# Reordering the down products of a two-layer MLA/GLA trunk's MLPs: the fifth sum second, the fourth sum fifth, one addition at high priority

## The chip, the core and the metric

The kernel runs on one core of a Trainium2 chip. The metric is the device time of one execution in microseconds (us). Three runs of the kernel before gave 1045.85 us as their median (1045.75 to 1047.25). The profile shows one further execution with its engines: PE is TensorE (matmul), PEld its weight loads, DVE is VectorE, ACT is ScalarE, POOL is GpSimd, SP is SyncE, which here issues DMAs only. Each engine works through its own instructions in a fixed order and waits on semaphores for the others.

## The reference

The reference is a decoder trunk of two layers on 512 tokens of width 1024, all in float32: layer 0 mixes with multi-head latent attention (MLA), layer 1 with gated linear attention (GLA), and each is followed by an MLP with a squared ReLU.

```
for i in range(DEPTH):                                  # DEPTH = 2
    x = x + mixer_i(rms_norm(x, norm_mix[i]))
    x = x + sq_relu_mlp(rms_norm(x, norm_mlp[i]), mlp_w_up[i], mlp_w_down[i])
return rms_norm(x, final_norm)

def sq_relu_mlp(xn, w_up, w_down):                      # 1024 -> 4096 -> 1024
    return jnp.square(jax.nn.relu(xn @ w_up)) @ w_down
```

The change lies in the two MLPs alone.

## The kernel before, in words

**Products.** Every float32 product is made of three fast matmuls: each operand is split into a rounded high part (ACT, line 110, or 844 with a sign) and a low part, the rest (DVE, line 113, or 845 with a sign), and high*high, high*low and low*high are added in PSUM. A weight block (`piece`, tiles `wh` and `wl`, four buffers each) costs ACT and DVE one instruction of 1024 columns each; a block of hidden values (`parts_of_quad`) one of 512 columns each. The hidden parts live in four rooms that are used in turn: the parts split as number n overwrite those split as number n-4, so that split waits until the product that read them is through.

**Seven products for eight.** The function `mlp` cuts the 4096 hidden columns into eight blocks (NB) of 512. The up and the down product of a block are 2 by 2 block products (halves of the width and of the tokens), done with seven block products each, from sums and differences of the quadrants, in place of eight. An up product is 24 matmuls of 256 columns (line 962), a down product 12 matmuls of 512 columns (line 971). The first block's up product is plain; then come seven steps, each doing the seven down products of block b and the seven up products of block b+1: one `step` (b = 0), in which ups and downs alternate, and six `step_in_halves` (b = 1 to 6, the middle steps), with seven ups and then seven downs. With two MLPs this makes two first steps and twelve middle steps.

**The down products.** With hidden quadrants q11, q12, q21, q22, DVE first makes q12 = q22 - q12 and q11 = q11 + q12. The results go to five sums in SBUF (`S11, S12, SU, S21, S5`). In a middle step of the kernel before the downs stand in this order: (1) q11 with d11; (2) the fourth sum: S21 += (q11 - q21) with d22; (3) q21 with d12, then S11 += e; (4) -q11 with d11 + ds1; (5) the fifth sum: S5 += (q11 - q22) with ds1; (6) q22 with d12, then S12 += e (line 1153); (7) q12 with ds3, then SU += d (line 1156). Products 2 and 5 (`onto`) copy their sum into two PSUM banks and back on ACT (line 1094). In `step` the later downs stand in a list at line 1084: -q11, q22, q12 (`down_12`), the fifth sum (`down_5`), the fourth (`down_21`).

**Loads.** When a product has read its weights for the last time, the step calls `after(name)`, and that issues the next block's DMA into the same tile: SP loads it, and for A2, S1, dS1 and dS3 POOL then adds a second block into it with an accumulating DMA (lines 940 and 951). In the last step of the second MLP `after` is `at_the_end`: it loads the last block's down weights and the final gain's row, rounds two of those weight tiles (`rounded(0)`), and adds S5 onto S12 (line 1199).

**What sets the order.** The order on the engines is not the order of the source. A planner walks the program with its own durations; whenever an engine is free it takes the ready instruction that stands first in the source (one under `tc.high_priority()` goes ahead of all others). Tiles of one tag are given out in the order of the source: a `tmp` (six buffers) or a `set` that is written later in the source is not given out before those ahead of it.

**The end.** After the last step of the second MLP, S12 is copied to PSUM (line 1248), the last hidden block is split (line 1250), the other two weight tiles are rounded (line 1253), the final gain is scaled by -0.5 (line 1255, DVE, 1024 columns), and `row` (line 1279) makes 96 matmuls in eight rows, the first of which accumulate onto the copy of S12. Only then do the final norm and the stores follow.

```
down_product(e, d12, p22, False)                    # sixth down of a middle step
DVE.tensor_tensor(S12, e, S12, ALU.add)             # line 1153
after("d12")
down_product(d, ds3, parts_of_quad(q12), False)     # seventh
...
loaded = {1: two_banks("e")}
ACT.activation(loaded[1], S12, AF.Copy)             # line 1248
```

Of the kernel before, what the change touches and what calls it, by code (L numbers as in the profile page):

```python
# [50 lines left out]
def trunk_kernel(ctx: ExitStack, tc: tile.TileContext, t_in: dict, out: bass.AP):  # L51
# [763 lines left out]
    def mlp(layer, nrm, nxt=None):  # L815
# [148 lines left out]
        def down_product(t, a, parts, start):  # L964
            wh, wl = piece(a, 2, 512)
            for tt in range(2):
                o = t[tt] if isinstance(t, list) else t[:, tt * 512 : (tt + 1) * 512]
                for k in range(2):
                    xh, xl = cut(parts, slice(None), slice(k * TH + tt * P, k * TH + (tt + 1) * P))
                    for n, (x_, w_) in enumerate(((xh, wh[:, k]), (xh, wl[:, k]), (xl, wh[:, k]))):  # L970
                        PE.matmul(o, x_, w_, start=start and k == 0 and n == 0, stop=k == 1 and n == 2, skip_group_check=True)  # L971


        def step(b, q, r, after):
            opening = nxt is not None
            (q11, q12), (q21, q22) = q

            def begun(src):
                t = two_banks("e")
                ACT.activation(t, src, AF.Copy)  # L980
                return t

            def add(total, t):
                if opening:
                    ACT.activation(total, t, AF.Copy)
                else:
                    DVE.tensor_tensor(total, t, total, ALU.add)

            def onto(tag, total, a, parts, fresh=False):
                t = two_banks(tag)  # L990
                if not fresh:
                    ACT.activation(t, total, AF.Copy)
                down_product(t, a, parts, fresh)
                ACT.activation(total, t, AF.Copy)

            A1, A2, s1 = W["A1"], W["A2"], W["S1"]
            a11, a12, s3, a22 = A1[:, :KH], A1[:, KH:], A2[:, :KH], A2[:, KH:]
            d11, d12, ds1, ds3, d22 = (W[n] for n in ("d11", "d12", "dS1", "dS3", "d22"))

            z = bank("u")  # L1000
            up_product(z, a11, "11", True)
            y = bank("u")
            ACT.activation(y, z, AF.Copy)

            d = two_banks("d")
            down_product(d, d11, parts_of_quad(q11), True)
            if opening:
                ACT.activation(S11, d, AF.Copy)
            e = two_banks("e") if opening else begun(d)

            up_product(y, a12, "21", False)
            finish(y, 0, 0, r)
            DVE.tensor_tensor(a11, s1, a11, ALU.add)

            down_product(e, d12, parts_of_quad(q21), opening)
            DVE.tensor_tensor(S11, e, S11, ALU.add)
            DVE.tensor_tensor(d11, ds1, d11, ALU.add)
            DVE.tensor_tensor(q12, q22, q12, ALU.subtract)
            DVE.tensor_tensor(q11, q11, q12, ALU.add)

            part = {"e": e}

            def down_11():
                down_product(d, d11, parts_of_quad(q11, -1.0), False)
                part["e"] = begun(d)
                DVE.tensor_tensor(d12, d11, d12, ALU.add)
                after("d11")

            def up_t2():
                up_product(z, a11, "T2", False)  # L1030
                u = part["u"] = tmp()
                ACT.activation(u, z, AF.Copy)
                DVE.tensor_tensor(a12, a11, a12, ALU.add)

            def up_t1():
                w = part["w"] = bank("u")
                up_product(w, s1, "T1", True)
                w2 = part["w2"] = bank("u")
                ACT.activation(w2, w, AF.Copy)
                after("S1")  # L1040

            def down_22():
                e = part["e"]
                down_product(e, d12, parts_of_quad(q22), False)
                add(S12, e)
                after("d12")

            def down_12():
                down_product(d, ds3, parts_of_quad(q12), False)
                add(SU, d)  # L1050
                after("dS3")
                DVE.tensor_tensor(q22, q22, q11, ALU.subtract)

            def up_22():
                w = part["w"]
                up_product(w, a12, "22", False)
                c = tmp()
                DVE.tensor_tensor(c, w, part["u"], ALU.add)
                finish(c, 0, 1, r)
                after("A1")  # L1060

            def up_t3():
                up_product(z, s3, "T3", False)
                v = tmp()
                ACT.activation(v, z, AF.Copy)
                c = tmp()
                DVE.tensor_tensor(c, part["w2"], v, ALU.add)
                finish(c, 1, 1, r)

            def down_5():  # L1070
                onto("e", S5, ds1, parts_of_quad(q22, -1.0), True)
                after("dS1")
                DVE.tensor_tensor(q21, q21, q11, ALU.subtract)

            def down_21():
                onto("d", S21, d22, parts_of_quad(q21, -1.0), opening)
                after("d22")

            def up_t4():
                up_product(z, a22, "T4", False)  # L1080
                finish(z, 1, 0, r)
                after("A2")

            for product in (up_t2, down_11, up_t1, down_22, up_22, up_t3, down_12, up_t4, down_5, down_21):
                product()

        def step_in_halves(b, q, r, after):
# [32 lines left out]
            c = tmp()  # L1120
            DVE.tensor_tensor(c, w2, v, ALU.add)
            finish(c, 1, 1, r)
            up_product(w, a12, "22", False)
            c = tmp()
            DVE.tensor_tensor(c, w, u, ALU.add)
# [4 lines left out]
            after("A2")  # L1130

            d = two_banks("d")
            down_product(d, d11, parts_of_quad(q11), True)
            e = copied(two_banks("e"), d)
            DVE.tensor_tensor(d11, ds1, d11, ALU.add)
            DVE.tensor_tensor(q12, q22, q12, ALU.subtract)
            DVE.tensor_tensor(q11, q11, q12, ALU.add)
            p21 = parts_of_quad(q21)
            DVE.tensor_tensor(q21, q21, q11, ALU.subtract)
            onto(S21, d22, parts_of_quad(q21, -1.0))  # L1140
            after("d22")
            down_product(e, d12, p21, False)
            DVE.tensor_tensor(S11, e, S11, ALU.add)
            down_product(d, d11, parts_of_quad(q11, -1.0), False)
            e = copied(two_banks("e"), d)
            DVE.tensor_tensor(d12, d11, d12, ALU.add)
            after("d11")
            p22 = parts_of_quad(q22)
            DVE.tensor_tensor(q22, q22, q11, ALU.subtract)
            onto(S5, ds1, parts_of_quad(q22, -1.0))  # L1150
            after("dS1")
            down_product(e, d12, p22, False)
            DVE.tensor_tensor(S12, e, S12, ALU.add)
            after("d12")
            down_product(d, ds3, parts_of_quad(q12), False)
            DVE.tensor_tensor(SU, d, SU, ALU.add)
# [34 lines left out]
        def at_the_end(name):  # L1191
            if name in ("d11", "S1", "d12", "dS3"):
                i = len(last_raw)
                t = by_k(comb(home[name]), 2)
                k0 = (NB - 1) * FB + i % 2 * 256
                SP.dma_start(t, w_dn[k0 : k0 + 256, i // 2 * 512 : (i // 2 + 1) * 512].rearrange("(k p) n -> p k n", p=P))
                last_raw.append(t)
            if name == "dS1":
                DVE.tensor_tensor(S12, S12, S5, ALU.add)
                t = comb(home[name])  # L1200
                SP.dma_start(t, t_in["fin_row"].to_broadcast([P, D]))
                gain.append(t)
                rounded(0)

        for b in range(NB - 1):
# [46 lines left out]
        DVE.tensor_tensor(SU, SU, S5, ALU.add)  # L1252
        rounded(1)
        gain = gain[0]
        DVE.tensor_scalar(gain, gain, -0.5, None, ALU.mult)
        stats = [sm(3) for _ in range(NT)]
        rows = {}
        for c in range(2):
            for th in (1, 0):
                total = (S11, S12, S21, SU)[2 * c + th]  # L1260
                if c == 0:
                    if th not in loaded:
                        loaded[th] = two_banks("d")
                        ACT.activation(loaded[th], total, AF.Copy)
                    o = loaded[th]
                for i in range(2):
                    cs = slice(i * 512, (i + 1) * 512)
                    if c:
                        o = bank("u")
                        ACT.activation(o, total[:, cs], AF.Copy, scale=-1.0)  # L1270
                    rows[2 * th + i, c] = total[:, cs], o if c else o[:, cs]

        def row(t, c):
            y, o = rows[t, c]
# [583 lines left out]
```

## Time and profile before

| | us |
|---|---|
| median of three runs | 1045.85 (1045.75 to 1047.25) |
| the profiled execution: its time | 1046.67 |
| the profiled execution: its span | 1044.9 |
| PE busy | 1035.0 (99%) |
| DVE busy | 876.9 (84%) |
| ACT busy | 696.8 (67%) |
| granted TensorE clock | 0.998 |

The span is the stretch from the first to the last instruction; 1.8 us of the execution's time lie around it. Times of instructions are counted from the span's start. The first MLP's first step begins at 206.79 and its middle steps run from 245.70 to 474.8; in the second MLP they begin at 745 and 785.91, and the last middle step ends at 1014.9. A line number names the place in the source; that of a helper (110, 113, 844, 845, 962, 971, 1094) stands for every caller.

### The profile page before, as it was taken

How to read it: one execution, taken by the hardware profiler on the slowest of the kernel's cores; microseconds unless marked ns; L12 is line 12 of the kernel's file. 1: busy time of each engine (PE TensorE's matmuls, PEld its weight loads, DVE VectorE, ACT ScalarE, POOL GpSimd, SP SyncE). 2: the span in 40 equal slices, each digit the busy share in tenths (PEclk: the TensorE clock that was granted, in tenths of full speed). 3: DMA queues.
4: the chain of work that ended last, by engine and by line, in shares of the span. 5: the costliest groups of instructions: out<-in, count | busy, mean ns of one | idle time of the engine just before them, and what ended most of it. 6: DMA issues, size and time to landing. Idle time of an engine off the chain costs nothing.

```text
span 1044.9 us, 15747 instructions
## 1 busy us (share of the span) xinstructions
PE 1035.0 (99%) x5966; PEld 903.9 (87%) x5966; DVE 876.9 (84%) x1340; ACT 696.8 (67%) x1122; POOL 114.3 (11%) x128
## 2 busy tenths in 40 slices
PE   9999999999999999999999999999999999999997
PEld 8788888899899899898888888888889989989986
DVE  7889977988989989989687399469798999898993
ACT  8667754577776776785445566555677677677784
POOL 8400010301101101000000000000011111110000
PEclk9999999999999999999999999999999999999999
DMA  7401235769878778644212222165488778778422
GB/s 232 122 21 41 81 95 147 224 166 215 216 191 202 178 203 202 161 136 126 77 55 82 87 74 75 48 162 147 95 241 201 185 202 198 194 191 191 111 81 81
DMA packets 120717, 149.98 MB, mean 144 GB/s; under 512 B 9568, under 2 KB 86368, under 8 KB 120512
## 3 DMA queue, kind: packets, MB, share of 16 engines
q1 hardware_dynamic: 96144, 117.76, 35.4%
q0 software_dynamic: 22400, 29.36, 18.0%
q10 hardware_dynamic: 2096, 1.84, 0.6%
q8 instruction: 47, 0.77, 0.3%
q14 instruction: 30, 0.25, 0.1%
HBM read 144.49 MB, written 4.19 MB: 142 GB/s over the span
## 4 chain that ended last, share of the span: by engine, by line
PE 94%; DVE 3%; ACT 2%; issue 0%; DMA 0%; ACTq 0%; SPq 0%; DVEq 0%
PE ps L971 25%; PE ps L962 25%; PE ps L118 10%; PE ps L120 10%; PE ps L119 10%; PE ps L1279 2%; PE ps L1240 2%; PE ps L1499 1%; PE ps L135 1%; PE ps L421 1%; PE ps L1626 1%; DVE wl L113 1%; PE ps L1766 0%; PE ps L1549 0%; PE ps L684 0%
## 5 line engine op out<-in xcount | busy, mean ns | idle before, releaser
L971 PE MATMUL ps<-wh,set 128*128 128x512 f32 x784 | 245.7, 390 | 0.3 <-ACT set L110 0.3
L110 ACT ACTIVATE wh<-wraw 128x1024 fp32r<-128x1024 f32 x139 | 146.4, 1056 | 110.2 <-PE ps L119 42.6
L113 DVE TENSOR_TENSOR wl<-wraw,wh 128x1024 fp32r<-128x1024 f32 x139 | 169.7, 1222 | 39.0 <-ACT wh L110 38.7
L971 PEld LDWEIGHTS ps<-wh,set 128*128 128x128 f32 x784 | 147.0, 188 | 30.7 <-ACT set L110 0.7
L962 PE MATMUL ps<-T,wh 128*128 128x256 f32 x896 | 154.9, 275 | 0.0
L971 PE MATMUL ps<-wl,set 128*128 128x512 f32 x392 | 152.6, 389 | 0.0
L113 DVE TENSOR_TENSOR wl<-comb,wh 128x1024 fp32r<-128x1024 f32 x112 | 136.8, 1221 | 18.5 <-ACT wh L110 18.3
L110 ACT ACTIVATE wh<-comb 128x1024 fp32r<-128x1024 f32 x112 | 118.3, 1057 | 47.6 <-issue 28.7
L962 PEld LDWEIGHTS ps<-T,wh 128*128 128x128 f32 x896 | 135.4, 188 | 0.4
L962 PE MATMUL ps<-T,wl 128*128 128x256 f32 x448 | 123.4, 275 | 0.0
L962 PE MATMUL ps<-set,wh 128*128 128x256 f32 x672 | 117.1, 276 | 0.0
L118 PE MATMUL ps<-set,wh 128*128 128x512 f32 x280 | 109.7, 392 | 0.0
L119 PE MATMUL ps<-set,wh 128*128 128x512 f32 x280 | 109.6, 392 | 0.0
L120 PE MATMUL ps<-set,wl 128*128 128x512 f32 x280 | 109.3, 391 | 0.0
L962 PEld LDWEIGHTS ps<-set,wh 128*128 128x128 f32 x672 | 102.6, 188 | 1.3
L962 PE MATMUL ps<-set,wl 128*128 128x256 f32 x336 | 92.7, 276 | 0.0
L971 PEld LDWEIGHTS ps<-wl,set 128*128 128x128 f32 x392 | 73.6, 188 | 14.7
L962 PEld LDWEIGHTS ps<-T,wl 128*128 128x128 f32 x448 | 84.1, 188 | 0.1
L962 PEld LDWEIGHTS ps<-set,wl 128*128 128x128 f32 x336 | 63.1, 188 | 0.0
L120 PEld LDWEIGHTS ps<-set,wl 128*128 128x128 f32 x280 | 52.6, 188 | 11.1
L119 PEld LDWEIGHTS ps<-set,wh 128*128 128x128 f32 x280 | 52.6, 188 | 11.1 <-DVE set L750 0.2
L118 PEld LDWEIGHTS ps<-set,wh 128*128 128x128 f32 x280 | 52.6, 188 | 10.7
(415 smaller groups left out, 2015.4 us busy)
## 6 DMA issues: line engine op xcount, KB each, us to landing
comb<-in_mlp_w_down_dram SPq DMA_DIRECT2D x74, 512.0 KB, 4.1
wraw<-in_mlp_w_up_dram SPq DMA_DIRECT2D x18, 1024.0 KB, 5.6
comb<-in_mlp_w_down_dram POOLq DMA_DIRECT2D x28, 512.0 KB, 6.5
wraw<-in_mlp_w_up_dram SPq DMA_DIRECT2D x28, 512.0 KB, 5.6
wraw<-in_gla_w_in_dram SPq DMA_DIRECT2D x12, 1024.0 KB, 5.2
comb<-in_mlp_w_up_dram SPq DMA_DIRECT2D x14, 512.0 KB, 4.4
comb<-in_mlp_w_up_dram POOLq DMA_DIRECT2D x14, 512.0 KB, 6.4
wraw<-in_mlp_w_up_dram POOLq DMA_DIRECT2D x14, 512.0 KB, 7.6
```

What stands on the lines that cost most here:

```text
L110: order(ACT.activation(hi, src, AF.Copy))
L113: lo_eng.tensor_tensor(lo, src, f(hi), ALU.subtract)
L118: PE.matmul(psum, wh, xh, start=start, stop=False)
L119: PE.matmul(psum, wh, xl, start=False, stop=False)
L120: PE.matmul(psum, wl, xh, start=False, stop=stop)
L135: PE.transpose(psum, src, ident[: src.shape[0], : src.shape[0]])
L421: PE.matmul(p, w[:, i, j * P : (j + 1) * P], x, start=start, stop=stop)
L962: PE.matmul(o, a_, x_, start=start and j == 0 and k == 0 and n == 0, stop=k == KH - 1 and n == 2, skip_group_check=True)
L971: PE.matmul(o, x_, w_, start=start and k == 0 and n == 0, stop=k == 1 and n == 2, skip_group_check=True)
L1240: PE.matmul(p, a, x, start=False, stop=k == 3 and n == 2, skip_group_check=True)
L1279: PE.matmul(o, a, b_, start=False, stop=k == 3 and n == 2, skip_group_check=True)
L1499: PE.matmul(p[:, t - t0], k[:, t * P : (t + 1) * P], moving[:, t], start=True, stop=True)
```

## The change

It has five parts, in the two MLPs:

1. In `step_in_halves` the fifth sum's product becomes the second down and the fourth sum's the fifth, with their `after("dS1")` and `after("d22")`. The fifth sum's factor is no longer made in place (q22 -= q11, then split with the sign -1): q11 - q22 is written to a new `tmp` tile `less` and split plainly. The splits for the first three downs and the three DVE instructions that they need (q12, q11, `less`) move up in the source, ahead of the sixth up product. The turns of the rooms change with the order: p1, p5, p2, -q11, q11 - q21, q22, q12.
2. The addition S12 += e after the sixth down stands under `tc.high_priority()`.
3. In `step` the list at the end of the function is reordered: `down_5` stands where `down_12` stood and the reverse; the split of -q11 is called ahead of `up_t2`; q22 -= q11 moves into `down_22`; the fourth sum uses the PSUM tile `e`.
4. In `at_the_end`, `rounded(0)` moves from the name dS1 to the name d22, so it stays behind the fifth down.
5. The scaling of the final gain moves behind the copies of the sums to PSUM.

```
@@ step
-            part = {"e": e}
+            part = {"e": e, "p11": parts_of_quad(q11, -1.0)}
             def down_11():
-                down_product(d, d11, parts_of_quad(q11, -1.0), False)
+                down_product(d, d11, part["p11"], False)
...
                 down_product(e, d12, parts_of_quad(q22), False)
+                DVE.tensor_tensor(q22, q22, q11, ALU.subtract)
                 add(S12, e)
...
-                onto("d", S21, d22, parts_of_quad(q21, -1.0), opening)
+                onto("e", S21, d22, parts_of_quad(q21, -1.0), opening)
...
-            for product in (up_t2, down_11, up_t1, down_22, up_22, up_t3, down_12, up_t4, down_5, down_21):
+            for product in (up_t2, down_11, up_t1, down_22, up_22, up_t3, down_5, up_t4, down_12, down_21):
@@ step_in_halves
             finish(c, 1, 1, r)
+            p1 = parts_of_quad(q11)
+            DVE.tensor_tensor(q12, q22, q12, ALU.subtract)
+            DVE.tensor_tensor(q11, q11, q12, ALU.add)
+            less = tmp()
+            DVE.tensor_tensor(less, q11, q22, ALU.subtract)
+            p5 = parts_of_quad(less)
+            p2 = parts_of_quad(q21)
             up_product(w, a12, "22", False)
...
-            down_product(d, d11, parts_of_quad(q11), True)
+            down_product(d, d11, p1, True)
             e = copied(two_banks("e"), d)
             DVE.tensor_tensor(d11, ds1, d11, ALU.add)
-            DVE.tensor_tensor(q12, q22, q12, ALU.subtract)
-            DVE.tensor_tensor(q11, q11, q12, ALU.add)
-            p21 = parts_of_quad(q21)
+            onto(S5, ds1, p5)
+            after("dS1")
+            down_product(e, d12, p2, False)
+            DVE.tensor_tensor(S11, e, S11, ALU.add)
             DVE.tensor_tensor(q21, q21, q11, ALU.subtract)
-            onto(S21, d22, parts_of_quad(q21, -1.0))
-            after("d22")
-            down_product(e, d12, p21, False)
-            DVE.tensor_tensor(S11, e, S11, ALU.add)
             down_product(d, d11, parts_of_quad(q11, -1.0), False)
             e = copied(two_banks("e"), d)
             DVE.tensor_tensor(d12, d11, d12, ALU.add)
             after("d11")
-            p22 = parts_of_quad(q22)
-            DVE.tensor_tensor(q22, q22, q11, ALU.subtract)
-            onto(S5, ds1, parts_of_quad(q22, -1.0))
-            after("dS1")
-            down_product(e, d12, p22, False)
-            DVE.tensor_tensor(S12, e, S12, ALU.add)
+            onto(S21, d22, parts_of_quad(q21, -1.0))
+            after("d22")
+            down_product(e, d12, parts_of_quad(q22), False)
+            with tc.high_priority():
+                DVE.tensor_tensor(S12, e, S12, ALU.add)
@@ at_the_end
                 gain.append(t)
+            if name == "d22":
                 rounded(0)
@@ the end of mlp
-        DVE.tensor_scalar(gain, gain, -0.5, None, ALU.mult)
         stats = [sm(3) for _ in range(NT)]
...
                     rows[2 * th + i, c] = total[:, cs], o if c else o[:, cs]
+
+        DVE.tensor_scalar(gain, gain, -0.5, None, ALU.mult)
```

More of the change, by code (lines that the diff above doesn't have):

```diff
@@ L1147, in step_in_halves @@
             after("d11")
-            p22 = parts_of_quad(q22)
-            DVE.tensor_tensor(q22, q22, q11, ALU.subtract)
-            onto(S5, ds1, parts_of_quad(q22, -1.0))
-            after("dS1")
-            down_product(e, d12, p22, False)
-            DVE.tensor_tensor(S12, e, S12, ALU.add)
+            onto(S21, d22, parts_of_quad(q21, -1.0))
[3 more added lines that the diff above has]
+                DVE.tensor_tensor(S12, e, S12, ALU.add)
             after("d12")
```

## The prediction

> **What bounds the kernel now.** I read the page first (busy shares and the chain that ended last), then the chain in order of time, to see where it leaves PE.
>
> ```profile
> span 1044.9 us, 15747 instructions
> PE 1035.0 (99%) x5966; PEld 903.9 (87%) x5966; DVE 876.9 (84%) x1340; ACT 696.8 (67%) x1122; POOL 114.3 (11%) x128
> PE 94%; DVE 3%; ACT 2%; issue 0%; DMA 0%; ACTq 0%; SPq 0%; DVEq 0%
> ```
>
> ```profile
> 209.68 2.54 PE ps L971 x11
> ...
> 212.79 1.01 ACT xT L1008
> ...
> 214.78 1.23 DVE wl L113
> 216.00 0.61 DVE tmp L859
> 216.64 0.64 ACT set L860
> 217.27 0.53 ACT set L110
> 217.84 0.72 PE ps L971 x2
> ...
> 322.18 19.09 PE ps L962 x168
> 341.27 19.07 PE ps L971 x84
> ...
> 1011.47 1.22 DVE xT L1199
> ...
> 1013.20 0.69 DVE comb L1255
> 1013.89 1.14 DVE xT L1153
> 1015.06 1.04 ACT ps L1248
> 1016.14 22.34 PE ps L1279 x96
> ```
>
> PE is 99% busy and 94% of the chain. In a middle step the chain never leaves PE: 168 up matmuls in 19.09 us (0.114 each, 2.73 a product), 84 down matmuls in 19.07 (0.227 each, 2.72 a product). In the two MLPs it leaves PE in the first step and at the end. The stretches of one step each say the same; columns are length, then busy us of PE, PEld, DVE, ACT, POOL.
>
> ```profile
> 206.79:245.70 38.91, 38.76 (x253) 35.11 (x252) 32.46 (x38) 28.50 (x38) 5.99 (x5) 1.00 0.75 185
> 322.02:360.18 38.16, 38.16 (x253) 34.85 (x252) 35.04 (x39) 28.25 (x40) 4.98 (x4) 1.00 0.76 196
> ```
>
> A middle step is 38.16 us with PE busy for all of it. So the change can win nothing in the twelve middle steps; it can only lose there. DVE has 38.16 - 35.04 = 3.1 us to spare in each. The first step takes 38.91, 0.75 more. What can be won is there and at the end.
>
> **Part 1 of the change, middle steps: forecast 0.** No matmul is added or removed. On DVE `less` takes the place of the subtraction q22 -= q11 (one of 512 columns for another), and a plain split that of a signed one. So DVE's 35.04 us stay. What moves is the time at which the parts can be made.
>
> ```profile
> 338.71 0.69 DVE L859 SCALAR_TENSOR_TENSOR tmp<-tmp,rstd 128x512 f32<-128x512 f32 x1
> ...
> 343.38 1.22 DVE L113 TENSOR_TENSOR wl<-comb,wh 128x1024 fp32r<-128x1024 f32 x1
> ...
> 351.10 0.68 DVE L845 SCALAR_TENSOR_TENSOR set<-set,set 128x512 fp32r<-128x512 f32 x1
> ```
>
> ```profile
> 343.63 0.61 PE L971 MATMUL ps<-wh,set 128*128 128x512 f32 x2
> ...
> 351.80 0.61 PE L971 MATMUL ps<-wh,set 128*128 128x512 f32 x2
> ```
>
> Each row of PE holds the last matmul of a down and the first of the next, so the second down begins at 343.86 and the fifth at 352.02. Before, the fifth's low part (line 845, 351.10 to 351.78) ends 0.7 us before its first use, the third matmul at 352.02 + 2 x 0.227 = 352.48: its room was held until the third product was through. After, the turns of the rooms follow the order of the products, so every split finds its room free at least three products (8 us) ahead. That takes a tight place away, at no gain, since PE never waited there. The new tight place is `less`: it is a `tmp`, so it comes behind the `tmp` of the fifth up's finish (338.71). At the earliest it starts at 339.32; with 0.69 for it, some 0.63 for the high part on ACT and 0.69 for the low part it is done at 341.4, and PE wants the low part at 344.31. I take 0; the other bound is the third rival below.
>
> The moved loads:
>
> ```profile
> comb<-in_mlp_w_down_dram SPq DMA_DIRECT2D x74, 512.0 KB, 4.1
> ```
>
> ```profile
> 351.78 1.19 POOL L951 DMA_DIRECT2D comb<-in_mlp_w_down_dram  x1 [11.15 <-DVE set L845]
> ```
>
> dS1's load goes up three places on SP, past d22's and d11's, and its adding DMA on POOL from 351.78 to some 342, past nothing (A2's stays ahead of it, dS3's behind). d22's load goes back three places and is wanted three products later. Each is wanted a whole step, 38 us, after its issue against 4.1 us to landing (some 10 with POOL's). Cost 0; without that cover each late us would be a us per step.
>
> **Part 3, the first steps: forecast -0.8.**
>
> ```profile
> 212.25 0.63 ACT L110 ACTIVATE set<-set 128x512 fp32r<-128x512 f32 x1 [1.10 <-PE ps L971]
> ...
> 214.78 1.23 DVE L113 TENSOR_TENSOR wl<-comb,wh 128x1024 fp32r<-128x1024 f32 x1 [1.17 <-ACT wh L110]
> ...
> 214.92 0.28 PE L962 MATMUL ps<-set,wl 128*128 128x256 f32 x1
> ...
> 217.41 0.28 PE L962 MATMUL ps<-T,wh 128*128 128x256 f32 x1
> 217.84 0.50 PE L971 MATMUL ps<-wh,set 128*128 128x512 f32 x1 [0.15 <-ACT set L110]
> ...
> 218.64 0.66 PE L971 MATMUL ps<-wh,set 128*128 128x512 f32 x2
> 758.06 0.50 PE L971 MATMUL ps<-wh,set 128*128 128x512 f32 x1 [0.18 <-ACT set L110]
> ```
>
> The split at 212.25 is that of q12, far ahead of its use: it took the room of the first down at the moment that product ended, and pushed back the copy at 212.79, the weight split behind it, the `wl` at 214.78 for which DVE sat idle 1.17, the finish (216.00), and by that q21's high part (217.27), for which PE waits at 217.84. In the new order that room goes to the split of q22 - q11, which cannot be ready so early (it needs q22's own split). The copy then starts at 212.25, 0.54 earlier, and the chain behind it by as much, until PE's own pace binds: 24 matmuls would have ended 2 x 0.114 after 217.55, and the third down matmul, at 218.64 now, could start at 217.55 + 0.23 + 2 x 0.227 = 218.23. That is 0.41, in each MLP (758.06 shows the same wait, 0.18 beside 0.15): 0.8. Bounds: 0 if another instruction fills the slot, below nothing by 0.4 in each if it is a longer one (a weight split, 1.0 for 0.6); 1.5 at most, the 0.75 over a middle step, twice. I take 0.8, the nearest to its row. The other swaps in the list cost 0: when down_5 runs, its parts, its `ds1` and the PSUM tile `e` have been ready for several products, as those of down_12 were.
>
> **Parts 2, 4 and 5, the end: forecast -1.3.**
>
> ```profile
> 1010.86 0.69 DVE L113 TENSOR_TENSOR set<-comb,set 128x512 fp32r<-128x512 f32 x1 [0.31 <-ACT set L110]
> ...
> 1012.60 0.69 DVE L113 TENSOR_TENSOR set<-set,set 128x512 fp32r<-128x512 f32 x1
> ...
> 1013.80 1.22 DVE L1153 TENSOR_TENSOR xT<-ps,xT 128x1024 f32<-128x1024 f32 x1
> ```
>
> ```profile
> 1011.20 0.63 ACT L110 ACTIVATE set<-set 128x512 fp32r<-128x512 f32 x1
> ...
> 1012.72 1.16 ACT L110 ACTIVATE set<-comb 128x512 fp32r<-128x512 f32 x2
> ```
>
> ```profile
> 1014.64 0.39 PE L971 MATMUL ps<-wh,set 128*128 128x512 f32 x1
> 1016.14 0.73 PE L1279 MATMUL ps<-set,set 128*128 128x512 f32 x2 [1.11 <-ACT ps L1248]
> ```
>
> The seventh down ends at 1014.64 + 0.23 = 1014.87; the rows of line 1279 start at 1016.14, 1.27 late, and their first two matmuls take 0.73 where two take 0.61 in the flow: 1.4 in all. They wait for the copy of S12 (1248), that for S12 += e (1153, at 1013.80), though the sixth down ended at about 1012.2 (1014.87 less 2.72). DVE had no arrears at 1010.86 (idle 0.31 before it). Ahead of 1153 stood S12 += S5 (1.13 from start to start), a hidden split (0.60) and the gain (0.61). After the change S12 += S5 follows the second down, 8 us earlier, and the gain's row, loaded at dS1, lands as much earlier, so that the planner can put the scaling into any idle slot of DVE. The hidden split then waits for its high part (1011.83) and ends its turn at 1012.47; S12 += e runs from there to about 1013.65, ACT is through with its two roundings at 1013.88, the copy ends at 1014.9, and PE goes on at 1014.95: 1.2 won, and the slow first pair with it, 1.3. If the gain still stands in front, 1013.08 and 1015.40: 0.75. Below nothing: `less` and its split bring 1.3 us more DVE work into the down phase, which has idle slots of as much; a cost of 0.5 is the bound. The high priority by itself is worth nothing that I can see: 1153 already stood first in the source among what was left, and was late only because the planner took other work until it held the sixth down to be through.
>
> **Sum.** 0 - 0.8 - 1.3 = -2.1. Against the profiled execution: 1046.67 becomes 1044.6, span 1044.9 becomes 1042.8. The median of the three runs lies 0.8 below the profiled execution; from 1045.85 I forecast 1043.7.
>
> **Rivals.** (1) Only one of the two stalls goes, because the planner fills the freed place with other work: 1045.85 - 0.8 to 1.3, so 1044.5 to 1045.1. For it: the planner is greedy and has its own durations; against: the freed places are narrow, 0.5 and 1.1 us. (2) Nothing shows: the same instructions stand before S12 += e, or new small waits eat the gain: 1045.4 to 1046.3. For it: the high priority changes no rank; against: the two instructions that stood in the way do move. (3) The other side: `less` is late in the middle steps. Line 1125, a weight split, both finishes and line 1146 stand on DVE from 339.32 to 343.38; if `less` comes behind them, its low part is done at 345.4, 1.1 after PE wants it, twelve times: +13, 1059; half the delay beyond the turning point gives 1052. It decides once `less` starts after 342.3 (344.31 less 2.0). Against it: in the source `less` stands ahead of line 1125. (4) S12 += e, drawn ahead, stands at the head of DVE before the sixth down is through, and what is queued behind it (weight splits) waits too. The row at 214.78 shows such a wait: 1.17 idle. DVE can lose 3.1 us in a step before PE starves, and a down is 2.72, so it decides only if the addition is placed more than a product too early; at 4.1 us early, 1.0 in each of twelve steps, 1058.
>
> On (4) the Trainium skill, "TensorE: Matmul & The Clock Gate", section "Architectural detail", says that the queues of ACT and DVE are strictly first in, first out. This trace agrees as far as it shows (1.17 idle with a finish behind whose product's last matmul began at 214.92). By that rule alone an early addition would block DVE, the 1058 above; by the row's 3.1 us to spare it costs nothing.
>
> **Chances.** Both stalls go (the forecast) 0.52, its own range 1043.0 to 1044.4; rival 1 0.17; rival 2 0.09; rival 3 0.18; rival 4 0.04. 0.2% is 2.1 us, about what a measurement of this kernel can tell from no change: below 1043.76 or above 1047.94. Of the forecast's 0.52 I put 0.38 below 1043.76 (little is left over if both go whole), so faster 0.38; within 0.14 + 0.17 + 0.09 = 0.40; slower 0.22. The range leaves out rivals 3 and 4 and little else: 1042.9 to 1047.0.
>
> **What would show it.** Right: no wait of line 1279 on line 1248 over 0.2 us, line 1153 starting by 1012.7 less what was won before; no wait of line 971 on line 110 in the first steps; middle steps of 38.16. Wrong: middle steps longer than 38.3 with PE waiting for a `set` at the second down (rival 3), or for `wl` (rival 4).

## The result and the profile after

The changed kernel takes 1047.64 us (median of 12 runs, 1046.1 to 1052.11); the kernel before took 1046.1 in the same session (12 runs, 1045.6 to 1047.34). The ratio is 1.0023 with a 95% interval of 1.0015 to 1.0032: slower by some 0.23%, where 0.2% faster was forecast. Beside the median the spread has changed: four of the changed kernel's runs lie at 1049 to 1052, and no run of before lies above 1047.4, here or beside a later experiment, except one slow one of 1287.51 at a granted clock of 0.752, which no comparison uses.

Three lines of the page of the changed kernel (span, busy times, shares of the chain that ended last), then the end of that chain; the profiled execution took 1047.52 us. Columns of the chain: start, length, what.

```profile
span 1045.8 us, 15773 instructions
PE 1034.9 (99%) x5966; PEld 903.4 (86%) x5966; DVE 876.6 (84%) x1340; ACT 696.5 (67%) x1122; POOL 112.9 (11%) x128
PE 93%; DVE 2%; ACT 2%; DMA 1%; issue 0%; SPq 0%; DVEq 0%; ACTq 0%
```

```profile
1009.99 1.15 DVE wl L113
...
1011.15 4.35 DMA comb<-in_mlp_w_down_dram
...
1016.06 1.02 ACT ps L1252
...
1017.12 22.27 PE ps L1284 x96
```

The work is the same (PE 1034.9 busy, 1035.0 before). What is new is a DMA in the chain that ends last: a weight split on DVE, then the load of the last weight tile, then the copy of S12 (line 1252, 1248 before), then the last product.

The stretches of the two first steps and of one middle step (length, busy us of PE, PEld, DVE, ACT, POOL; granted clock, DMA share, GB/s), first the changed kernel:

```profile
207.14:246.14 39.00, 38.80 (x254) 35.13 (x253) 32.43 (x38) 28.31 (x38) 5.97 (x5) 1.00 0.73 184
322.46:360.62 38.16, 38.16 (x254) 34.85 (x253) 34.97 (x39) 28.24 (x39) 5.11 (x5) 1.00 0.78 193
745.41:786.51 41.10, 40.90 (x272) 36.96 (x270) 33.56 (x38) 27.70 (x36) 4.99 (x4) 1.00 0.65 168
```

and the second MLP's first step in the kernel before:

```profile
744.89:785.91 41.02, 40.84 (x272) 36.97 (x270) 34.48 (x40) 29.08 (x37) 4.99 (x4) 1.00 0.64 167
```

Middle steps: 38.16 as before. First steps: 39.00 for 38.91 and 41.10 for 41.02, so 0.09 worse each in place of 0.41 better.

The end, on ACT, PE, DVE and SP's queue (in this order; the number in brackets is idle time and what ended it):

```profile
1012.90 0.63 ACT L110 ACTIVATE set<-comb 128x512 fp32r<-128x512 f32 x1 [1.71 <-DMA comb<-in_mlp_w_down_dram]
...
1015.52 0.63 ACT L110 ACTIVATE set<-comb 128x512 fp32r<-128x512 f32 x1 [0.95 <-DMA comb<-in_mlp_w_down_dram]
1016.06 1.01 ACT L1252 ACTIVATE ps<-xT 128x1024 f32<-128x1024 f32 x1
```

```profile
1015.24 0.39 PE L971 MATMUL ps<-wh,set 128*128 128x512 f32 x1
1017.12 1.20 PE L1284 MATMUL ps<-set,set 128*128 128x512 f32 x4 [1.49 <-ACT ps L1252]
```

```profile
1001.61 0.69 DVE L1276 TENSOR_SCALAR comb<-comb 128x1024 f32<-128x1024 f32 x1
...
1004.09 1.22 DVE L1202 TENSOR_TENSOR xT<-xT,sum 128x1024 f32<-128x1024 f32 x1
...
1009.90 1.22 DVE L113 TENSOR_TENSOR wl<-comb,wh 128x1024 fp32r<-128x1024 f32 x1
...
1012.95 1.23 DVE L1156 TENSOR_TENSOR xT<-ps,xT 128x1024 f32<-128x1024 f32 x1 [0.62 <-PE ps L971]
```

```profile
1011.15 0.37 SPq L1199 DMA_DIRECT2D comb<-in_mlp_w_down_dram  x1
```

S12 += e (line 1156) does start as soon as the sixth down ends, at 1012.95; it is through by 1014.18. But the copy of S12 stands on ACT behind the rounding of the last block's last weight tile, and that waits for its DMA until 1015.52. The seventh down ends at 1015.24 + 0.23 = 1015.47, PE goes on at 1017.12: 1.65 late, 1.27 before. In the kernel before that load went out at 1008.84, 5.8 us ahead of the seventh down's last matmul (1014.64):

```profile
1008.84 0.37 SPq L1196 DMA_DIRECT2D comb<-in_mlp_w_down_dram  x1
```

In the changed kernel it goes out 4.1 ahead, when the seventh down's weight split (the `wl` at 1009.90) has released the tile.

That makes 0.4 at the end and 0.2 in the first steps, against medians 1.5 apart. The experiments look for the rest.

### The profile page after: what moved, and what is told of

The parts are those of the page before. It is cut to its first block, busy times and chain, and to the rows that moved or that the text cites. A ratio compares the mean times of both kernels' runs of the same rounds, so it can differ in the third digit from the quotient of the medians.

```text
span 1045.8 us, 15773 instructions
## 1 busy us (share of the span) xinstructions
PE 1034.9 (99%) x5966; PEld 903.4 (86%) x5966; DVE 876.6 (84%) x1340; ACT 696.5 (67%) x1122; POOL 112.9 (11%) x128
## 4 chain that ended last, share of the span: by engine, by line
PE 93%; DVE 2%; ACT 2%; DMA 1%; issue 0%; SPq 0%; DVEq 0%; ACTq 0%
PE ps L971 25%; PE ps L962 25%; PE ps L118 10%; PE ps L120 10%; PE ps L119 10%; PE ps L1284 2%; PE ps L1244 2%; PE ps L1504 1%; PE ps L135 1%; PE ps L421 1%; DVE wl L113 1%; PE ps L1631 1%; DMA xT<-in_x_dram 1%; DMA comb<-in_mlp_w_down_dram 0%; PE ps L1554 0%
```

## The experiments

The kernel before was run beside each; times of different sessions differ by some tenths, so each is compared by its ratio to before in its own session. Two variants are no experiments, since the planner builds the very same program from them: the changed kernel without `tc.high_priority()`, and the changed kernel with the gain's scaling at its old place in the source. Parts 2 and 5 of the change are thus without effect; what happens at the end comes from the new order of the downs (part 1) and the hooks that move with it (part 4).

**The copy ahead of the last rounding (e1).**

```
-        ACT.activation(loaded[1], S12, AF.Copy)
+        moved = ACT.activation(loaded[1], S12, AF.Copy)
...
-        rounded(1)
+        rounded(1, (0,))                   # third tile
+        with tc.issue_after(moved.ins):    # on ACT behind the copy
+            rounded(1, (1,))               # fourth tile
```

> The changed kernel with one instruction moved: the copy of S12 to PSUM goes ahead of the rounding of the last weight tile on ACT, nothing else. Theory A (the loss sits at the end: that rounding waits for its DMA, and the copy and PE behind it): the copy starts at about 1014.2 and PE's first row of the last product within 0.3 us of the seventh down's end, where it was 1.65 late; the median falls by 1.4 to 1.8 from 1047.64, to 1045.8 to 1046.2, level with the kernel before, and the single runs of 1049 to 1052 go. Theory B (the loss sits elsewhere, in the first steps or in loads of the middle steps): the wait at the end goes as well, but the median stays at 1046.8 or more and runs above 1049 stay.

1046.32 us (11 runs, 1045.29 to 1047.55), before 1045.89; ratio 1.0004 (0.9996 to 1.0013). Its ACT rows:

```profile
1013.02 0.62 ACT L110 ACTIVATE set<-comb 128x512 fp32r<-128x512 f32 x1
1013.54 1.01 ACT L1252 ACTIVATE ps<-xT 128x1024 f32<-128x1024 f32 x1
1014.49 0.61 ACT L110 ACTIVATE set<-comb 128x512 fp32r<-128x512 f32 x1
```

```profile
1014.30 0.39 PE L971 MATMUL ps<-wh,set 128*128 128x512 f32 x1
1014.60 1.66 PE L1286 MATMUL ps<-set,set 128*128 128x512 f32 x6
```

One instruction moved, and PE goes on within 0.1 of the seventh down's end. The median is a tenth above the forecast range and some 1.4 below the changed kernel's (1047.64, and 1047.77 in e4), and no run is above 1047.6. Theory A holds for the largest part: that one place on ACT costs the median some 1.4 us.

**The third and fourth tile loaded one product earlier (e2).**

```
-            if name in ("d11", "S1", "d12", "dS3"):
+            if name in ("d11", "S1", "d12", "d22"):
```

> The changed kernel with the last block's third and fourth weight tile loaded one product earlier each: the loads follow d22 and d12 in place of d12 and dS3, so that the last load is issued about 1.7 us earlier (1009.45 in place of 1011.15) into another tile. Theory A: landed by about 1013.8, no rounding waits for a DMA behind 1014, the copy of S12 ends by 1015.5 and PE is at most 0.4 late: 1045.8 to 1046.3. Theory B: 1046.8 or more, runs above 1049 stay.

1046.35 (12 runs, 1045.78 to 1050.95); ratio 1.0012 (1.0001 to 1.0022). The trace has PE 0.3 late at the end, so the median fits theory A to within 0.1. Three runs at 1048.9 to 1051 stay, as theory B had it: the last load is not all that makes runs long.

**The first step as before (e3; with the list, the split of -q11, the subtraction and the PSUM tile go back too), and the changed kernel once more (e4).**

```
-            for product in (up_t2, down_11, up_t1, down_22, up_22, up_t3, down_5, up_t4, down_12, down_21):
+            for product in (up_t2, down_11, up_t1, down_22, up_22, up_t3, down_12, up_t4, down_5, down_21):
```

> The changed kernel with the first step (one per MLP) as in the kernel before; middle steps and end as changed. Theory A: the two first steps cost the same in either order (their wait at the second down is 0.4 in both), so the time stays within 0.3 of 1047.6, and the wait at the end is still there. Theory B (the new order of the first step costs what the medians differ by beyond the end's 0.4): 1046.4 to 1046.8.

> The changed kernel once more, for a second trace beside the three others. Theory A: whatever the time is, the stretches up to the last step agree with the first trace within 0.3 us once the start is taken off, and what differs between the executions is the landing of the last load, and with it the start of the last product's first row. Theory B: differences of 0.5 us or more inside the MLPs ahead of the end.

e3: 1048.28 (7 runs), ratio 1.0021 (1.0011 to 1.0032). e4: 1047.77 (12 runs, 1045.94 to 1051.29), ratio 1.0018 (1.0009 to 1.0028). By the median e3 lies 0.5 above e4 and outside theory A's 0.3, but the intervals of their ratios overlap almost wholly: the order of the first step makes no difference that the times can tell. The traces tell one of some 0.1 in each MLP (38.90 and 41.03 in e3, 39.02 and 41.08 in e4). Against theory A as worded, both traces show a second wait ahead of the end, in the ups of the last middle step. ACT and PE of e4, and ACT of the kernel before at the same place:

```profile
980.98 1.16 ACT L110 ACTIVATE set<-comb 128x512 fp32r<-128x512 f32 x2 [2.37 <-DMA comb<-in_mlp_w_down_dram]
```

```profile
983.62 0.50 PE L962 MATMUL ps<-T,wh 128*128 128x256 f32 x2 [0.98 <-ACT ps L1094]
```

```profile
979.40 1.16 ACT L110 ACTIVATE set<-comb 128x512 fp32r<-128x512 f32 x2 [1.14 <-DMA comb<-in_mlp_w_down_dram]
```

This is the last block's first tile, loaded into the place of S1 and rounded by the planner at once, in both kernels, ahead of the step's weight splits. The loads of the kernel before and of the changed kernel:

```profile
974.73 0.37 SPq L1196 DMA_DIRECT2D comb<-in_mlp_w_down_dram  x1
975.73 0.37 SPq L1199 DMA_DIRECT2D comb<-in_mlp_w_down_dram  x1
```

Before, the load is issued 1.98 us ahead of the step's first matmul (974.73 against 976.71), and the rounding starts 2.70 after it; PE does not wait. In the changed kernel the load is issued 1.6 ahead (975.73 against 977.31), since the weight split on DVE that releases the place starts 2.83 ahead of the step in place of 3.23. In the traces with the new order of the downs that do not hold it back, the rounding starts 1.9 (e2) to 4.2 (e3) after the step's start, and between 2.7 and 3.0 PE begins to wait.

**The first tile's rounding held back (e5).**

```
             if name == "d22":
-                rounded(0)
+                with tc.issue_after(mark[0].ins):   # the third up's copy on ACT
+                    rounded(0)
```

> The changed kernel; in the last middle step the roundings of the last block's first weight tile stand behind the third up product's copy on ACT, some 6 us later than now, where they wait for the tile's DMA (idle 1.06, 2.37 and 2.58 us in three traces) with the step's weight splits queued behind them. Theory A (two late transfers, each with its own price): PE's wait of 1.0 to 1.2 us in the last step's ups, seen in two of four traces of this order, is gone, the median falls by 0.3 to 0.8, to 1046.8 to 1047.3, and the wait of 1.5 at the end with its single runs above 1049 stays. Theory B (the runs above 1049 come from this first tile): no run above 1048.3, median 1046.8 or less.

1047.44 (11 runs, 1046.44 to 1049.3); ratio 1.0014 (1.0006 to 1.0023). The ups run without a wait, 19.08 us. The median is 0.1 above theory A's range, and the gain over e4 is too small for the intervals; two runs above 1048.3 rule out theory B. The profiled execution, 1048.78, shows what a wait at the end can do beyond its length. Its chain, and PE in the 4 us behind the wait (length, busy, granted clock, DMA):

```profile
1010.27 4.87 DMA comb<-in_mlp_w_down_dram
...
1016.76 23.92 PE ps L1288 x96
```

```profile
1016.75:1020.75 4.00, 3.99 (x12) 0.67 0.00 0
```

PE had waited 2.16 us. Behind that the granted clock falls, matmuls start 0.427 us apart where they start 0.227 apart otherwise, and the 96 matmuls take 23.92 in place of 22.3: a wait of 2.2 costs 3.8.

**The mended kernels (e6, e11) and two variants of before (e7, e8).** The edit that they share, in `step`:

```
+            p21 = parts_of_quad(q21)
             up_product(y, a12, "21", False)
             finish(y, 0, 0, r)
...
-            down_product(e, d12, parts_of_quad(q21), opening)
+            down_product(e, d12, p21, opening)
```

e6 is the changed kernel with this, e1's and e5's edits; e11 adds e2's to these; e7 is the kernel before with this edit alone; e8 is e7 with the gain's scaling and one split of the last block queued on DVE behind S12 += e:

```
-            DVE.tensor_tensor(S12, e, S12, ALU.add)
+            mark[0] = DVE.tensor_tensor(S12, e, S12, ALU.add)
...
+            with tc.issue_after(mark[0].ins) if (h, th) == (1, 1) else nullcontext():
                 hid[h, th] = parts_of_quad(q[h][th])
...
+        with tc.issue_after(mark[0].ins):
             DVE.tensor_scalar(gain, gain, -0.5, None, ALU.mult)
```

> The changed kernel with the copy of S12 ahead of the last tile's roundings, the first tile's roundings held back, and in the first step the split of q21 taken ahead of the finish that stands before it in the source. Theory A: the copy gives 1.3 (measured), the held tile 0.3 to 0.8, the first steps 0.4 each: 1044.6 to 1045.2 beside 1045.9 of the kernel before. Theory B (what the first steps wait for is not the turn of q21's split): 1045.4 to 1046.0, with PE still waiting 0.4 in each first step.

> The kernel before with the split of q21 taken ahead of the finish in the first step, nothing else. Theory A (PE waits there for q21's high part, which stands behind the finish since tiles are given out in source order): the two waits at the second down go, 0.4 each: 1045.1. Theory B (PE's pace or the planner gives the gain back elsewhere in the step, as it did with the change): 1045.7 to 1046.1.

> The kernel before with q21's split as in the run before this one, and at the end the gain's scaling and one split of the last block queued on DVE behind S12 += e. Theory A (S12 += e was late by these two instructions, 1.2 us, and its copy on ACT is held up by nothing else, since the last load is issued at 1008.8 there): PE's wait of 1.27 ahead of the last product shrinks to under 0.2, and the time is 1.1 to 1.3 below the run before this one: about 1043.9. Theory B (another instruction or a transfer holds the copy): no gain over the run before this one.

> The mended kernel with, beside the other three edits, the third and fourth weight tile loaded one product earlier each. Theory A: no rounding at the end waits for a transfer, PE's 0.2 ahead of the last product goes, the 96 matmuls take 22.3 to 22.6: 1045.0 to 1045.4, 0.7 to 1.1 under the kernel before in the same session. Theory B: nothing is left at the end that transfers set: the same as the mended kernel within 0.1.

| | median us (runs) | ratio to before | PE late at the end |
|---|---|---|---|
| e6 | 1045.39 (11) | 0.9994 (0.9985 to 1.0002) | 0.4 |
| e7 | 1045.64 (11) | 0.9996 (0.9987 to 1.0005) | 1.27 |
| e8 | 1045.7 (11) | 0.9997 (0.9988 to 1.0006) | 0.28 |
| e11 | 1044.8 (11) | 0.999 (0.9981 to 0.9999) | 0.30 |

The first steps of e7, in the first and the second MLP:

```profile
206.43:244.96 38.53, 38.53 (x254) 35.05 (x252) 32.37 (x38) 28.40 (x38) 5.84 (x5) 1.00 0.73 187
744.23:784.98 40.75, 40.66 (x272) 36.94 (x270) 34.47 (x40) 28.85 (x37) 4.99 (x4) 1.00 0.67 173
```

So the wait in the first steps was the place of q21's split behind the finish (theory A): 38.91 becomes 38.53, and 41.02 becomes 40.75. Beside the kernel before in the same session (1046.22) e7 is 0.6 faster where 0.8 was expected, and e6 0.8 where 0.7 to 1.3 was; both intervals reach 1. e8, for which a further 1.1 to 1.3 was expected, won 1.0 us at PE's restart and lost it again: in its trace the copies of lines 1269 and 1275 come 0.3 and 0.4 late for the rows behind, and between the last matmul and the end 0.65 more passes than in e7, since the planner put the square of the last row ahead of another row's scaling on ACT. e11, 0.2 below its forecast range, is the one version here whose interval lies wholly below the kernel before, and only just (0.1%, up to 0.9999): first step 38.53, no wait for a DMA at the end, 22.3 for the 96 matmuls, and its runs keep to 1044.26 to 1046.49.

```profile
1013.34 0.39 PE L971 MATMUL ps<-wh,set 128*128 128x512 f32 x1
1013.86 2.35 PE L1291 MATMUL ps<-set,set 128*128 128x512 f32 x9
```

**The last load twice (e9).**

```
-                SP.dma_start(t, w_dn[k0 : k0 + 256, ...
+                for _ in range(2 if i == 3 else 1):
+                    SP.dma_start(t, w_dn[k0 : k0 + 256, ...
...
-        ACT.activation(loaded[1], S12, AF.Copy)
...
         rounded(1)
+        with tc.high_priority(), tc.issue_after(waited[0].ins):   # the fourth tile's rounding
+            ACT.activation(loaded[1], S12, AF.Copy)
```

> The changed kernel with the last weight tile loaded twice in a row into the same place, and the copy of S12 kept behind that tile's rounding on ACT: the wait made some 3.5 to 4 us longer, nothing taken away. Theory A (the single runs at 1049 to 1052 are late landings of this load, and a PE wait of 2 us or more also halves the granted clock for some 3 us, as in the trace with the first tile held, where matmuls stood 0.427 us apart in place of 0.227 behind a wait of 2.0): PE waits 4.5 to 6 us, the granted clock falls to about 0.5 behind it, the 96 matmuls take 23.9 in place of 22.3, and the time is 1047.6 + 3.5 to 4 + 1.6, 1052 to 1053.5, with every run above 1051. Theory B (the wait costs its own length only): 1050.5 to 1051.6, the 96 matmuls 22.3.

1050.36 (4 runs, 1049.78 to 1051.49); ratio 1.0046 (1.003 to 1.0061).

```profile
1018.05 1.22 PE L1292 MATMUL ps<-set,set 128*128 128x512 f32 x2 [2.65 <-ACT ps L1275]
```

```profile
1018.00:1022.00 4.00, 3.95 (x11) 0.63 0.07 27
```

The length of the wait was forecast wrong, 2.8 us (1018.05 less 1015.01 + 0.23) in place of 4.5 to 6: the planner drew the copy of the other half, S11 (line 1275), and its rows ahead, so PE did not stand until the tile had landed. The time is therefore below both theories' ranges; 1.15 more wait than in the first trace and 1.4 more in the 96 matmuls account for 2.5 of the 2.7 from 1047.64. The clock did as theory A has it: 0.63 behind the wait, 23.67 us for the 96 matmuls.

**The gain held back (e10), S12 += S5 left out (e16).**

```
-        DVE.tensor_scalar(gain, gain, -0.5, None, ALU.mult)
+        with tc.issue_after(mark[0].ins):     # mark[0]: S12 += e
+            DVE.tensor_scalar(gain, gain, -0.5, None, ALU.mult)
```

```
             if name == "dS1":
-                DVE.tensor_tensor(S12, S12, S5, ALU.add)
```

> The changed kernel with the gain's scaling (0.6 us on DVE, at 1001.61 in the changed kernel) queued behind S12 += e. Theory A (the last load goes out late because DVE does S12 += S5 and the gain ahead of the weight splits that free the load's tile): the splits and the last load come up to 0.6 us earlier, the wait at the end falls from 1.5 to about 1.0 and the median by 0.5, to 1047.1. Theory B (another instruction holds the seventh down's weight split): no change in the load's issue, 1047.4 to 1047.9, or more where the gain then stands in the rows' way.

> The changed kernel without S12 += S5 (left out: the first half of the width of the second half of the tokens lacks the fifth sum). Theory A (the addition, which the new order draws to the second down, stands on DVE ahead of the sixth and seventh downs' weight splits, and the last load waits for the seventh's): the last load is issued 1.1 us or more earlier against the last down matmul, at -5.2 to -5.8 in place of -4.1 us, no rounding waits for it behind the seventh down, and PE's wait at the end is under 0.6. Theory B (the seventh's split is late for another reason, as the run with the gain held back could not tell): the issue stays at -4.1.

e10: 1047.86 (11 runs), ratio 1.0021 (1.0012 to 1.003); the load is issued 4.1 us ahead of the last down matmul, as without the edit. The gain is not it (theory B); in its trace the edit costs 0.65 behind the last matmul, 7.08 us to the end in place of 6.43. e16, one run, whose result lacks the fifth sum in one quarter, took 1046.33 beside 1045.97 of before:

```profile
1008.82 1.22 DVE L113 TENSOR_TENSOR wl<-comb,wh 128x1024 fp32r<-128x1024 f32 x1
```

```profile
1010.07 0.37 SPq L1199 DMA_DIRECT2D comb<-in_mlp_w_down_dram  x1
```

```profile
1015.09 0.39 PE L971 MATMUL ps<-wh,set 128*128 128x512 f32 x1
1015.93 2.33 PE L1283 MATMUL ps<-set,set 128*128 128x512 f32 x9 [0.45 <-ACT ps L1251]
```

The load goes out 5.02 ahead of the last down matmul (4.1 with the addition), a little short of the 5.2 expected, and PE is 0.61 late in place of 1.65. Theory A, by one execution: the addition, which the new order draws forward to 1004.09, holds the weight split that releases the last tile. The remaining 0.8 to the kernel before's 5.8 was not tried.

**A long execution (e12 to e15).** The changed kernel unaltered, four single runs.

> The changed kernel once more, one look, to meet one of its long executions (1049 and above, about one in four). Theory A: a long one shows PE waiting over 2 us at the end for the rounding of the last load, or over 1 us in the last step's ups behind the first tile's, with the granted clock near half behind the wait; one near 1047.5 shows a wait of 1.2 to 1.7 at full clock. Theory B: a long one has its extra time elsewhere.

> As the run before this one, a further look: Theory A, extra time only behind the two late loads of the last block, with the clock halved after a wait over 2 us; Theory B, elsewhere.

> As the two runs before this one, a further look: Theory A, extra time only behind the two late loads of the last block, with the clock halved after a wait over 2 us; Theory B, elsewhere.

> As the three runs before this one, a further look: Theory A, extra time only behind the two late loads of the last block, with the clock halved after a wait over 2 us; Theory B, elsewhere.

With the first trace and e4 there are six of the changed kernel. "Tile 1" is the start of its rounding after the step's first matmul, "ups" the stretch of the last middle step's ups, "late" the time from the seventh down's end to the last product.

| | us | tile 1 | ups | late | 96 matmuls |
|---|---|---|---|---|---|
| first trace | 1047.52 | +2.68 | 19.08 | 1.65 | 22.27 |
| e4 | 1048.45 | +3.98 | 20.36 | 1.63 | 22.28 |
| e12 | 1046.70 | +2.65 | 19.08 | 1.28 | 22.27 |
| e13 | 1047.41 | +3.02 | 19.40 | 1.91 | 22.29 |
| e14 | 1049.93 | +2.99 | 19.34 | 2.17 | 23.88 |
| e15 | 1046.94 | +2.17 | 19.08 | 1.68 | 22.28 |

e14 is the long one. Its chain, and PE in the wait, behind it and further on:

```profile
1011.52 4.76 DMA comb<-in_mlp_w_down_dram
...
1016.84 1.02 ACT ps L1252
...
1017.90 23.88 PE ps L1284 x96
```

```profile
1015.90:1017.90 2.00, 0.00 (x1) 1.00 0.00 0
1017.90:1021.90 4.00, 4.00 (x11) 0.57 0.00 0
1021.90:1025.90 4.00, 4.00 (x19) 1.00 0.00 0
```

The load took 4.76 us against 4.35 in the first trace, and was issued 0.1 later against the last down matmul. That made the wait 2.17, and the clock at 0.57 for 4 us made it 1.6 dearer. Two smaller losses come to it: 0.26 in the ups, and 0.24 in the downs, where the last block's second tile, issued at 1001.19, had not landed before 1006.03 and held ACT idle for 1.16, with a copy that PE's weight loads wait for 0.35 later behind it. With them the trace is 2.6 longer than the first one, of which 0.2 is won ahead of the MLPs; the times are 2.4 apart. Theory A holds for the largest part of it, 2.4 of the 2.6 lying behind the two loads that it names.

## Why the prediction was wrong

The forecast was 1043.7 in a range of 1042.9 to 1047.0, with 0.22 for slower; it came out at 1047.64, outside the range.

**Part 1, middle steps, 0.** Right for the twelve steps themselves: 38.16, and `less` starts 17.30 us into the step, the earliest start that the working gave (339.32 less 322.02), so rival 3 did not come up. Wrong in what was said of the moved loads: "Each is wanted a whole step, 38 us, after its issue". In the last middle step of the second MLP the hooks load the last block's tiles, and the first and the last of these are wanted within some 4 us. These loads were not followed. The first tile's load goes out 0.4 later against the step's start and makes PE wait 0 to 1.3 us, on average 0.3 over the six traces.

**Part 3, first steps, -0.8.** The step that failed is "24 matmuls would have ended 2 x 0.114 after 217.55", PE's order of before. The rows of ACT moved the way that was forecast, but by less:

```profile
212.83 1.03 ACT L1008 ACTIVATE xT<-ps 128x1024 f32<-128x1024 f32 x1 [1.32 <-PE ps L971]
...
217.24 0.61 ACT L110 ACTIVATE set<-set 128x512 fp32r<-128x512 f32 x1
```

Counted from the step's start (207.14, 206.79 before), the copy of line 1008 begins 0.31 earlier in place of 0.54, and q21's high part 0.28. In PE's old order that would have been worth some 0.28, an estimate from these rows. But the planner moved three of the up matmuls that stood ahead of the down product into it, so PE came to its first down matmul 0.34 earlier, and waited as before:

```profile
217.43 0.28 PE L962 MATMUL ps<-T,wh 128*128 128x256 f32 x1
217.91 0.50 PE L971 MATMUL ps<-wh,set 128*128 128x512 f32 x1 [0.20 <-ACT set L110]
```

The step is 0.09 longer in each MLP. The diagnosis of the wait was right (e7 takes it away by q21's place alone, 0.38 and 0.27); the edit did not reach it.

**Parts 2, 4 and 5, the end, -1.3.** The DVE half came out: S12 += e starts at the sixth down's end, 0.62 idle before it. The step that failed is "ACT is through with its two roundings at 1013.88". It took the roundings from the rows of before, where their tile had landed. They wait for a load that S12 += S5, the very addition moved out of the way, makes late (e16: 0.9 of the 1.7 us by which it goes out later than before). The bound below nothing, 0.5, was made from DVE's work alone and had no DMA in it. Measured: 1.65 late in place of 1.27, 1.72 on average over the six traces, and in one of six the half clock on top. That the high priority is worth nothing was right: it moves no instruction.

**Rivals.** 3 and 4 did not come up; line 1156 waits once in its twelve places, 0.62 at the head of DVE's queue, and PE loses nothing by it that shows. The row at 214.78 that rival 4 rests on does not show a queue held up, since the finish behind it was not ready either; ACT at the end of the changed kernel does, where S12 was ready to be copied at 1014.18 and the copy began at 1016.06, behind a rounding that waited for its tile. "Nothing shows" comes nearest in time, for another reason. The mechanism that decided was not among them: an instruction on ACT waiting for a transfer, with the copy that PE needs queued behind it.

**The sum, by the six traces.** First steps 0.09 + 0.08, ups of the last step 0.3, the wait at the end 0.45 more, the half clock 1.6 in one of six, 0.3: 1.2 of the 1.5 to 1.9 between the medians. These terms are averages, and the averages of the first session's runs lie 2.4 apart (1048.6 and 1046.2), so more than that is left over; it is not placed. Runs of 1050 and above, apart from e9's, came in the changed kernel, e2 and e3, which all round the first tile at once; but so do e1 and e10, and none of their 22 runs reached 1050. No trace of a run above 1050 was met, so what makes them stays open.

## What to carry to other kernels

When work is drawn ahead on one engine, ask which buffer is released later by it, which load waits for that buffer, and what stands behind the load's first reader on its own queue; at this kernel's end a load was wanted within some four microseconds of its issue, not a step later. An order made by a planner is not a constant: a freed slot on one engine changes the order of the others, so a gain that rests on their old order needs a second look. A wait of PE has a second price once it is long enough for the clock.

## What the runs showed of the hardware

A wait of PE of 2.16 us (e5), 2.17 (e14) or 2.8 (e9) was followed by a stretch at a granted clock near one half (0.57 to 0.67 over the 4 us behind it, matmuls 0.427 us apart in place of 0.227), which cost 1.4 to 1.6 us beyond the wait; at 0.53 of the rate 1.6 lost make a stretch of 3.4 us. Waits up to 1.91 (e13) were not followed by one; whether the limit always lies between the two is not shown. The Trainium skill, "TensorE: Matmul & The Clock Gate", section "What's actually happening", tells of such a gate with two states, and puts the fall at one idle window of about 3.4 us or more, the window running freely. The half rate and its length of about one window agree with these traces; the wait that is enough was shorter here, 2.2 us.

The same 512 KB load at the same place took 3.98 us in e12, 4.35 in the first trace, 4.76 in e14 and 4.87 in e5; a schedule that leaves it 4.1 us is late by a different amount in each execution, and that shows as spread before it shows in the median. Executions also differ ahead of the change: with the same order of instructions up to there, the first step began at 206.79 in the trace of before and at 207.14 in that of the changed kernel, 0.35 apart; over the six traces of the changed kernel it began between 206.51 and 207.14.
